# Two PSUM banks kept by one pool through the whole program, and two of three score tiles moved into them

## The chip, the cores and the metric

The kernel runs on one core of one Trainium2 chip. The metric is the device time of one launch in microseconds; the kernel before takes 1682.73 us (median of three runs, 1681.79 to 1683.66). The core's engines are named as in the profile: PE does the matmuls (PEld is its loading of weights), DVE, ACT and POOL are the vector, scalar and GpSimd engines, SP issues most of the transfers. PSUM, into which PE accumulates, has eight banks of 128 partitions by 512 fp32 values.

## The reference

A bidirectional encoder of two layers runs with the same weights on two groups of tokens (512 and 256, here handled as T = 768 columns), width 1024, fp32.

```python
for i in range(DEPTH):
    h = rms_norm(x, norm_mix[i])
    if i % N_MIXERS == 0:
        x = x + window_attention(h, attn_w_qkv[j], attn_w_o[j], attn_sink[j], band_bias, in_window)
    else:
        x = x + short_conv(h, conv_w_in[j], conv_w[j], conv_w_out[j])
    h = rms_norm(x, norm_mlp[i])
    x = x + jnp.square(jax.nn.relu(h @ mlp_w_up[i])) @ mlp_w_down[i]
    gate = jax.nn.sigmoid(rms_norm(x, norm_ple[i]) @ ple_w_gate[i])
    x = x + (p[i] @ ple_w_proj[i]) * gate
return rms_norm(x, final_norm)
```

Layer 0 has the attention: 16 heads of 64 over 4 key/value heads, blocks of 128 queries that see up to three blocks of 128 keys (|distance| at most 128), a bias per head and distance, and a learned sink logit that enters the maximum and the denominator. Layer 1 has the gated convolution of width 3. The MLP is 4096 wide.

## The kernel before, in words

**Accuracy.** Every fp32 operand is split into a high part (ACT, L83) and the rest (DVE, L84), and a product is three matmul passes: high by high, high by rest, rest by high. In the names `whi`/`wlo`, `zhi`/`zlo` are the parts of a weight, `qh`/`ql` of the queries, `khh`/`kll` of the keys, `aos` those of the heads' outputs.

**Stages.** From 0 to 73 us the inputs are projected and normalized, and keys, queries of the first heads and values are made; the pool `psK` gives three two-bank tiles for the products and a tag "S" of two banks for small things: `bp` (the bias table), `rt` (a transpose) and the six blocks of values `vp` (L653 to L655, read by ACT at L658 and DVE at L659). Then `psK` closes, `psA` opens, and attention runs to 277 us. `psA` has one two-bank accumulator `mm` (two tags, `BM`=1), three banks for score tiles (`BS`=3), one for the output `O` and two for transposes. Then `psA` closes and the pool `ps` takes all eight banks for the rest, 1400 us: four under tag A, two under C, two under B. There each product needs two banks, `both()`, and `fresh()` picks the tag from "ACAB" by a counter, `shift`.

**Attention.** 24 units (4 key/value heads by 6 blocks of 128 tokens). In a unit each of four heads has a score tile S (PE, L708 and L709), which DVE reads once, adding the bias and taking the maximum (L710). ACT exponentiates (L730), DVE and ACT scale (L736, L738), PE transposes (pt, L743), ACT and DVE split the transposes (`ph` L751, `pl` L752), and PE multiplies them with the values into O (L753, L754), from which `heads` is made (L761). Beside the units PE does the products of 512 or 256 columns that later units need (L138): the queries of later heads, `keys1`, `projected` (inputs of the second layer) and the parts of the output projection that are ready (`first_output`, `second_output`, summed into `xa` at L777). Queries are scaled, split, and sent to their places by four DMAs for each pair of heads, issued by SP (L625).

**What sets the order.** In attention and ahead of it a list scheduler at build time decides in which order each engine's instructions stand; a tile's release (its bank's last reader) enters that decision. On the chip each engine then takes its own instructions in that fixed order, and waits on semaphores. From the head of the next stage on the order is as written. That stage begins with `first_head`: six products of the last heads' outputs (L129, `group2`), each with an add into x on DVE (L847); `first_tail` has two more and the four products `pj`, whose tags are written out as A, B, C, A.

Of the kernel before, what the change touches and what calls it, by code (L numbers as in the profile page):

```python
# [11 lines left out]
F32 = mybir.dt.float32  # L12
# [3 lines left out]
PSUM = bass.MemoryType.PSUM  # L16
DRAM = bass.MemoryType.DRAM

P = 128
# [8 lines left out]
NEG = -1e30  # L28
CH = 1024

BM, BS, BO, BT, BL = 1, 3, 1, 2, 5

NA = 1

# [13 lines left out]
def trunk_kernel(ctx: ExitStack, tc: tile.TileContext, a: dict, out: bass.AP):  # L48
# [6 lines left out]
    wp = ctx.enter_context(tc.tile_pool(name="wp", bufs=2))  # L55
    stat = ctx.enter_context(tc.tile_pool(name="stat", bufs=1))
    dram = ctx.enter_context(tc.tile_pool(name="dram", bufs=1, space=DRAM))

    act.preload_act_table_set(EXP_LN)
    tmp, turn, shift = None, 0, 0  # L60


    vec = const.tile([P, 7 * KB + 3 * KB], F32, name="vec")
# [39 lines left out]
    BANKS = {"A": 4, "C": 2, "B": 2}  # L103

    def bank(tag, name):
        return psum.tile([P, 512], F32, tag=tag, name=name, bufs=BANKS[tag])

    def fresh(name="mm", n=1, tag=None):

# [371 lines left out]
    def mixer_attention():  # L481
        s1, s2 = ExitStack(), ExitStack()
        psum = s2.enter_context(tc.tile_pool(name="psK", bufs=3, space=PSUM))
# [8 lines left out]
        def pair(j, name, dt=F32):  # L492
            return main.tile([P, 2, T], dt, tag=f"x{j}", name=name)
# [40 lines left out]
        with tc.manual_schedule(engines=order):  # L534
            w0 = wp.tile([P, CH], F32, name="wraw", bufs=3)
            p0 = []
            for k in range(2):
                c = slice(512 * k, 512 * k + 512)
                nc.sync.dma_start(w0[:, c], a["proj"][0, 0, :, c])
                t = big("p")  # L540
                nc.sync.dma_start(t[:], a["p"][0, :, k, :])
                p0.append(t)
            w1 = fetch(a["proj"][0, 1])
            nc.sync.dma_start(vec[:], a["vec"][:])
            for m in range(KB):
                nc.sync.dma_start(xin(m), a["x"][m])
            wk = fetch(a["w_k"][0])
            rb = ap.tile([32, HEADS], F32, name="rb", bufs=1)
            nc.sync.dma_start(rb[:], a["rel_bias"][:])
            oh = ap.tile([32, 512], F32, tag="bias", name="oh", bufs=4)  # L550
            nc.sync.dma_start(oh[:], a["onehot"][:])
            mk = ap.tile([HEADS, 512], F32, tag="bias", name="mk", bufs=4)
            nc.sync.dma_start(mk[:], a["mask"][:].broadcast_to([HEADS, 512]))
            nc.sync.dma_start(sink[:], a["sink"][:].broadcast_to([P, HEADS]))

            hi = wp.tile([P, CH], F32R, name="whi", bufs=2)
            lo = wp.tile([P, CH], F32R, name="wlo", bufs=2)
            part0 = [], []
            for k in range(2):
                c = slice(512 * k, 512 * k + 512)  # L560
                split(hi[:, c], lo[:, c], w0[:, c])
                ph, pl = slot(10 + k, "p0h"), slot(12 + k, "p0l")
                split(ph[:], pl[:], p0[k][:])
                part0[0].append(ph[:])
                part0[1].append(pl[:])
            w0 = blocks(hi[:], 2), blocks(lo[:], 2)
            w1 = weight(None, 2, raw=w1)
            for i in range(KB):
                step(0, i, (w0, w1)[i // 4], part0, "L", i % 2)
                norm.block(i, xin(i))  # L570
                if i == 3:
                    wk = weight(None, KB, raw=wk)
                    wq = [fetch(a["w_q"][0])]

            bp = psum.tile([P, 512], F32, tag="S", name="bp", bufs=2)
            pe.matmul(bp[:HEADS, :], lhsT=rb[:], rhs=oh[:], start=True, stop=True)
            brow = tmp.tile([HEADS, 512], F32, tag="t", name="brow")
            dve.tensor_tensor(brow[:], bp[:HEADS, :], mk[:], ALU.add)
            kps = list(products(terms_of(wk, xs)))
            wq[0] = weight(None, KB, raw=wq[0])  # L580
            ss = norm.sum_squares(psum)

        with s1:
# [44 lines left out]
                        )  # L628

            rc = ap.tile([P, T // P], F32, name="rc", bufs=1)  # L630
            rt = psum.tile([P, 512], F32, tag="S", name="rt", bufs=2)
            for n in range(T // P):
                pe.transpose(rt[:, n : n + 1], r[0:1, n * P : (n + 1) * P], ident[0:1, 0:1])
            dve.tensor_copy(rc[:], rt[:, : T // P])
# [11 lines left out]
                    parts += blocks(t[:, :m], m // 256)  # L646

            def values(n):
                ps = psum.tile([P, 512], F32, tag="S", name="vp", bufs=2)
                for k in range(KB):  # L650
                    xh, xl = (xs[i][k][:, n * P : (n + 1) * P] for i in range(2))
                    wh, wl = wv[0][k], wv[1][k]
                    pe.matmul(ps[:, :256], lhsT=xh, rhs=wh, start=k == 0, stop=False)  # L653
                    pe.matmul(ps[:, :256], lhsT=xh, rhs=wl, start=False, stop=False)
                    pe.matmul(ps[:, :256], lhsT=xl, rhs=wh, start=False, stop=k == KB - 1)  # L655
                src = ps[:, :256].rearrange("p (g d) -> p g d", g=KV)
                hi, lo = vv[:, n, :, 0, :], vv[:, n, :, 1, :]
                act.activation(hi, src, AF.Copy, scale=rc[:, n : n + 1])  # L658
                dve.scalar_tensor_tensor(lo, src, rc[:, n : n + 1], hi.bitcast(F32), ALU.mult, ALU.subtract)  # L659
# [24 lines left out]
            biases = {}  # L684
            bands(0)

            def attend(g):
                heads[g] = pair(g, "heads")
                if g < KV - 1:
                    bands(g + 1)  # L690
# [2 lines left out]
                for s in SEQS:  # L693
                    hi_blk = lo_blk + s // P
                    for n in range(lo_blk, hi_blk):
# [6 lines left out]
                        for hp in range(2):  # L702
                            L = ap.tile([P, 2, 384], F32, tag="L", name="L", bufs=BL)
                            for j in range(2):
                                h = REP * g + 2 * hp + j
                                S = psum.tile([P, 512], F32, tag="S", name="S", bufs=BS)
                                q = qst[h][:, n * P : (n + 1) * P]
                                pe.matmul(S[:, :w], lhsT=q, rhs=khh[g][:, k0 * P : k0 * P + w], start=True, stop=False)  # L708
                                pe.matmul(S[:, :w], lhsT=q, rhs=kll[g][:, k0 * P : k0 * P + w], start=False, stop=True)  # L709
                                dve.tensor_tensor_reduce(  # L710
                                    L[:, j, :w],
                                    S[:, :w],
                                    bias[hp][:, j, j0 : j0 + w],
                                    1.0,
                                    sink[:, h : h + 1],
                                    ALU.add,
                                    ALU.max,
                                    accum_out=mx[:, 2 * hp + j : 2 * hp + j + 1],
                                )
                            lg.append(L)  # L720
# [261 lines left out]
    def first_tail(norm, places, output, product, ws):  # L982
# [9 lines left out]
        norm.ready = True  # L992
        c = ws[1]
        m6, m7 = KB - 1, KB // 2 - 1
        ps = [output(m) for m in (m6, m7)]
        pjs.extend(product(m) for m in range(KB // 2))
        add(m6, ps[0], xa[m6])
        norm.plain_block(m6, x(m6))
# [931 lines left out]
```

## Time and profile before

| what | us |
|---|---|
| median of three runs | 1682.73 |
| lowest, highest | 1681.79, 1683.66 |
| the profiled execution | 1684.2 |
| its span, first to last instruction | 1682.2 |
| PE busy in the span | 1645.5 (98%) |
| DVE busy | 1411.9 (84%) |
| ACT busy | 905.8 (54%) |
| stage to 73.33 us | 73.33, PE busy 66.30 |
| attention, 73.33 to 276.85 | 203.52, PE busy 197.13 |
| the rest, from 276.85 | 1405.3, PE busy 1382 |

The profiled execution lies 1.5 us above the median, and 2.0 us of it lie around the span. The granted clock of PE is 0.996 over the span. The page of the profile gives busy time by engine; the groups of waits say for how long an engine's next instruction stood and what released it; the timeline gives single instructions with that idle time in brackets; a table of windows gives busy time and clock in stretches.

### The profile page before, as it was taken

To read this page: it belongs to the slowest core of one execution; us is meant where nothing else is said; L and a number is where in the kernel's file an instruction comes from. 1 tells how busy PE (TensorE), PEld (TensorE's weight loads), DVE (VectorE), ACT (ScalarE), POOL (GpSimd) and SP (SyncE) were. 2 spreads that over 40 slices of the span, in tenths; PEclk is the share of its full clock that TensorE was granted. 3 is DMA by queue.
4 is the path that set the end of the run, shared out by engine and by line. 5 is a ranking of instruction groups with operands and counts; after the bars stand their busy time and mean duration, and the time that the engine had idled before them with its cause. 6 is when DMAs were issued, how large, how long until landed. Compare 5 with 4: busy or idle time off the path is not lost.

```text
span 1682.2 us, 24112 instructions
## 1 busy us (share of the span) xinstructions
PE 1645.5 (98%) x9410; PEld 1586.8 (94%) x9410; DVE 1411.9 (84%) x2302; ACT 905.8 (54%) x1451; POOL 20.3 (1%) x46
## 2 busy tenths in 40 slices
PE   8999999999999999999999999999999999999996
PEld 6888788999999999999999999999999999999985
DVE  6598888899999999977788787768999898998776
ACT  6377756755555455545654334545555545554544
POOL 0211000000000000000000000000000000000000
PEclk9999999999999999999999999999999999999998
DMA  8755322411221222231312222121222122122222
GB/s 262 192 152 143 92 66 74 121 63 63 76 76 64 75 76 66 73 104 63 101 60 76 76 75 76 61 66 54 73 75 76 63 76 76 63 76 88 82 76 95
DMA packets 47107, 145.64 MB, mean 87 GB/s; under 512 B 6112, under 2 KB 9184, under 8 KB 46992
## 3 DMA queue, kind: packets, MB, share of 16 engines
q1 hardware_dynamic: 45168, 139.89, 26.1%
q0 software_dynamic: 1824, 4.20, 1.2%
q8 instruction: 74, 1.21, 0.3%
q14 instruction: 41, 0.34, 0.1%
HBM read 124.14 MB, written 10.48 MB: 80 GB/s over the span
## 4 chain that ended last, share of the span: by engine, by line
PE 58%; DVE 30%; ACT 7%; issue 3%; DMA 1%; SPq 0%; DVEq 0%; ACTq 0%
PE a L476 17%; PE mm L129 9%; PE mm L138 8%; PE b L476 4%; PE B L476 4%; PE C L476 3%; DVE t L362 3%; DVE wlo L455 3%; DVE y L1031 3%; PE gate L138 3%; DVE zlo L455 2%; DVE act L395 1%; PE pt L743 1%; DVE sum L412 1%; ACT y L1034 1%
## 5 line engine op out<-in xcount | busy, mean ns | idle before, releaser
L436 ACT ACTIVATE whi<-sum 128x1024 fp32r<-128x1024 f32 x67 | 70.5, 1053 | 150.7 <-PE a L476 146.8
L1034 ACT ACTIVATE y<-y 128x768 f32<-128x768 f32 x64 | 53.7, 840 | 135.5 <-DVE y L1031 135.5
L476 PE MATMUL a<-xs,whi 128*128 128x384 f32 x624 | 121.9, 337 | 2.4 <-DVE y L1279 1.7
L476 PEld LDWEIGHTS a<-xs,whi 128*128 128x128 f32 x624 | 110.0, 188 | 3.1 <-DVE y L1279 2.0
L476 PE MATMUL a<-t,zhi 128*128 128x384 f32 x536 | 109.1, 337 | 0.0
L476 PE MATMUL a<-t,whi 128*128 128x384 f32 x536 | 108.8, 336 | 0.0
L476 PE MATMUL b<-t,zhi 128*128 128x384 f32 x536 | 108.8, 336 | 0.0
L476 PE MATMUL a<-act,whi 128*128 128x384 f32 x448 | 96.5, 337 | 0.0
L476 PEld LDWEIGHTS a<-t,whi 128*128 128x128 f32 x536 | 94.9, 188 | 0.0
L476 PEld LDWEIGHTS a<-t,zhi 128*128 128x128 f32 x536 | 94.6, 188 | 0.2 <-ACT c L1752 0.2
L476 PEld LDWEIGHTS b<-t,zhi 128*128 128x128 f32 x536 | 94.8, 188 | 0.0
L455 DVE TENSOR_TENSOR wlo<-wraw,whi 128x1024 fp32r<-128x1024 f32 x70 | 85.3, 1218 | 7.6 <-ACT whi L436 7.6
L455 DVE TENSOR_TENSOR wlo<-sum,whi 128x1024 fp32r<-128x1024 f32 x67 | 81.9, 1222 | 8.9 <-ACT whi L436 8.9
L1312 DVE TENSOR_TENSOR x<-x,a 128x384 f32<-128x384 f32 x112 | 60.7, 552 | 33.8 <-PE a L476 33.5
L436 ACT ACTIVATE zhi<-sum 128x1024 fp32r<-128x1024 f32 x67 | 71.0, 1060 | 23.0 <-DVE sum L412 23.0
L138 PE MATMUL mm<-xs_mix,whi 128*128 128x512 f32 (+1 forms) x320 | 83.0, 342 | 0.0
L455 DVE TENSOR_TENSOR zlo<-sum,zhi 128x1024 fp32r<-128x1024 f32 x67 | 81.5, 1217 | 0.0
L476 PEld LDWEIGHTS a<-act,whi 128*128 128x128 f32 x448 | 79.8, 188 | 0.0
L436 ACT ACTIVATE whi<-wraw 128x1024 fp32r<-128x1024 f32 x72 | 75.7, 1051 | 6.2 <-PE C L476 6.2
L356 ACT ACTIVATE t<-y 128x768 fp32r<-128x768 f32 x56 | 47.1, 842 | 40.6 <-DVE y L347 29.9
L476 PE MATMUL a<-xs,wlo 128*128 128x384 f32 x312 | 67.1, 336 | 0.0
L455 DVE TENSOR_TENSOR vlo<-wraw,vhi 128x512 fp32r<-128x512 f32 x67 | 46.1, 689 | 24.8 <-ACT vhi L436 24.8
(338 smaller groups left out, 4503.7 us busy)
## 6 DMA issues: line engine op xcount, KB each, us to landing
wraw<-in_up SPq DMA_DIRECT2D x64, 512.0 KB, 3.5
wraw<-in_down SPq DMA_DIRECT2D x64, 512.0 KB, 3.5
wraw<-in_w_in SPq DMA_DIRECT2D x24, 512.0 KB, 3.5
wraw<-in_gate SPq DMA_DIRECT2D x16, 512.0 KB, 3.4
pj<-pjs SPq DMA_DIRECT2D x16, 384.0 KB, 3.8
wraw<-in_w_q SPq DMA_DIRECT2D x8, 512.0 KB, 4.5
wraw<-in_w_out SPq DMA_DIRECT2D x8, 512.0 KB, 3.4
x_in<-in_x SPq DMA_DIRECT2D x8, 384.0 KB, 7.3
```

What stands on the lines that cost most here:

```text
L129: pe.matmul(t, lhsT=w, rhs=x[:, o:e], start=first and i == 0 and j == 0, stop=last and i == n - 1 and j == 2)
L138: pe.matmul(ps[:, o:e], lhsT=w, rhs=x[:, o:e], start=i == 0 and j == 0, stop=i == n - 1 and j == 2,)
L356: act.activation(t[0][:], (self.q1, self.q2)[i][:], AF.Copy)
L362: dve.tensor_tensor(lo[:], (self.q1, self.q2)[i][:], hi[:].bitcast(F32), ALU.subtract)
L395: dve.tensor_tensor(lo[:], self.q2[:], hi[:].bitcast(F32), ALU.subtract)
L412: dve.tensor_tensor(a[:, 512:], a[:, :512], r2[:, 512:], ALU.add)
L436: act.activation(hi[:], src, AF.Copy)
L455: dve.tensor_tensor(lo[:], src, hi[:].bitcast(F32), ALU.subtract)
L476: pe.matmul(ps, lhsT=a, rhs=b, start=start and i == 0, stop=i == len(terms) - 1, skip_group_check=True)
L1031: dve.scalar_tensor_tensor(t[:, o:e], src, 0.0, r[:, o:e], op, ALU.mult)
L1034: act.activation(t[:], t[:], AF.Square)
L1312: dve.tensor_tensor(t[:, o : o + H], t[:, o : o + H], f, op)
```

## The change

A pool `psB` of two banks is opened at the start of the program and never closed. `bank("B", ...)` takes from it, so the later stages' pair B, the bias table, the transpose and the blocks of values lie there. In attention two of every three score tiles lie there too, and the third in a tag "S" of one bank of `psA`; `psK`, `psA` and `ps` have six banks each. In the first product stage `shift` starts at 2 in place of 0, so the products of `first_head` take the banks B A C A B A in place of C A B A C A, and the two of `first_tail` C A in place of B A. `shift` is then set back by 2, and the rest of the program has the banks that it had.

```diff
-BM, BS, BO, BT, BL = 1, 3, 1, 2, 5
+BM, BO, BT, BL = 1, 1, 2, 5
...
+    pair_of_banks = ctx.enter_context(tc.tile_pool(name="psB", bufs=2, space=PSUM))
...
-    tmp, turn, shift = None, 0, 0
+    tmp, turn, shift = None, 0, 2
...
     def bank(tag, name):
-        return psum.tile([P, 512], F32, tag=tag, name=name, bufs=BANKS[tag])
+        pool = pair_of_banks if tag == "B" else psum
+        return pool.tile([P, 512], F32, tag=tag, name=name, bufs=BANKS[tag])
...
-            bp = psum.tile([P, 512], F32, tag="S", name="bp", bufs=2)
+            bp = bank("B", "bp")
...
-            rt = psum.tile([P, 512], F32, tag="S", name="rt", bufs=2)
+            rt = bank("B", "rt")
...
             def values(n):
-                ps = psum.tile([P, 512], F32, tag="S", name="vp", bufs=2)
+                ps = bank("B", "vp")
...
+            scores = 0
+
+            def third():
+                return psum.tile([P, 512], F32, tag="S", name="S", bufs=1)
+
             def attend(g):
+                nonlocal scores
...
-                                S = psum.tile([P, 512], F32, tag="S", name="S", bufs=BS)
+                                S = third() if scores % 3 == 1 else bank("B", "S")
+                                scores += 1
...
+        nonlocal shift
         ps = [output(m) for m in (m6, m7)]
+        shift -= 2
         pjs.extend(product(m) for m in range(KB // 2))
```

No instruction is added or removed on any engine. POOL's order is the same; those of PE, DVE, ACT and SP differ inside attention alone. The numbers behind names below are the program's own and differ by three between the two kernels; the lines of the changed kernel are up to nine lower down (L717 is L708 of before).

At the turn from values to scores, at 73 us, PE's order is the same in both: the six blocks of values, two score tiles of two heads, then the queries of the second group. What differs is the read for which the first score waits. Before it is DVE's of the sixth and last block of values (the last read of `psK`), now DVE's of the fifth, since the pair's banks take turns and the first score follows the fifth block in its bank.

The first place shown is PE about 160 us, behind the product `projected` (`mm` from `p1`), where the first scores of the third group of heads stand (`q_1872` and `q_1875`, freshly sent, are `q_1875` and `q_1878` now). Before:

```order
L754 MATMUL O_1782<-pl_1800,vv_454 128x512 [waits DVE_49]
L138 MATMUL mm_1973<-p1_1313,whi_1942 128x256
L138 MATMUL mm_1973<-p1_1312,wlo_1943 128x256
L708 MATMUL S_2035<-khh_1385,q_1682 128x256 [waits DMAHW1_49,DMAHW0_49]
L709 MATMUL S_2035<-kll_1386,q_1682 128x256
L708 MATMUL S_2040<-khh_1385,q_1872 128x256 [waits DMAHW4_49,DMAHW3_49]
L709 MATMUL S_2040<-kll_1386,q_1872 128x256
L708 MATMUL S_2044<-khh_1385,q_1875 128x256 [waits DMAHW6_49,DMAHW5_49]
L709 MATMUL S_2044<-kll_1386,q_1875 128x256
L708 MATMUL S_2093<-khh_1385,q_1679 128x384 [waits DVE_49]
```

In the changed kernel, with some thirty rows left out in the middle:

```order
L717 MATMUL S_2096<-khh_1388,q_1682 128x384 [waits DVE_49]
L717 MATMUL S_2043<-khh_1388,q_1875 128x256 [waits DMAHW6_49,DMAHW5_49]
L718 MATMUL S_2043<-kll_1389,q_1875 128x256
L718 MATMUL S_2096<-kll_1389,q_1682 128x384
L140 MATMUL mm_1986<-p1_1315,whi_1945 128x512 [waits Activation_49]
...
L140 MATMUL mm_2012<-p1_1315,wlo_1946 128x256
L717 MATMUL S_2047<-khh_1388,q_1878 128x256 [waits DMAHW7_49,DMAHW0_49]
L718 MATMUL S_2047<-kll_1389,q_1878 128x256
```

The two scores that need freshly sent queries stood next to each other, and now the second stands behind more of `projected`.

The second place is DVE about 205 to 211 us, around the split of the finished heads (`aos` from `heads`; the first row of `aos` in a list is the half whose product PE has next). Before:

```order
L752 TENSOR_TENSOR pl_2421<-pt_2415,ph_2420 128x512 [waits Activation_49]
L710 ISA L_2500,mx_2499<-S_2505,bias_1398,sink_74 128x256
...
L710 ISA L_2509,mx_2499<-S_2510,bias_1403,sink_74 128x256
...
L710 ISA L_2509,mx_2499<-S_2514,bias_1403,sink_74 128x256 [waits PE_49]
...
L84 TENSOR_TENSOR aos_2562<-heads_769,aos_2561 128x768
L761 TENSOR_TENSOR heads_2018<-O_2403,ot_2426 64x2x128 [waits Activation_49]
...
L723 TENSOR_SCALAR nm_2518<-mx_2499 128x4 [waits DVE_49]
L725 TENSOR_TENSOR es_2520<-sink_74,mx_2499 128x4
L84 TENSOR_TENSOR aos_2566<-heads_769,aos_2565 128x768
```

In the changed kernel:

```order
L761 TENSOR_TENSOR pl_2424<-pt_2418,ph_2423 128x512 [waits Activation_49]
L85 TENSOR_TENSOR ql_2493<-qt_2439,qh_2492 128x768 [waits DMAHW1_49,DMAHW0_49,Activation_49]
L719 ISA L_2512,mx_2502<-S_2517,bias_1406,sink_77 128x256 [waits PE_49]
...
L770 TENSOR_TENSOR heads_2021<-O_2406,ot_2429 64x2x128 [waits Activation_49]
...
L732 TENSOR_SCALAR nm_2521<-mx_2502 128x4 [waits DVE_49]
L734 TENSOR_TENSOR es_2523<-sink_77,mx_2502 128x4
L85 TENSOR_TENSOR aos_2569<-heads_772,aos_2568 128x768
```

The first half of the heads (`aos_2565` now) has gone ahead of this piece, and the rest of the queries (`ql`) has come into it from ahead. On PE the product that reads `aos_2569` now follows at once on the one that reads `pl_2424`; before, six score matmuls and six product matmuls stood between their equals (`pl_2421` and `aos_2566`).

The third place is PE at the first product after attention (`mm` from `aos` and the weight's parts `zhi`, `zlo`). Before:

```order
L129 MATMUL mm_3342<-aos_3304,zhi_3338 128x384 [waits DMASW5_49,DMASW4_49,DMASW6_49,DMASW3_49,DMASW7_49,DMASW2_49,DMAHW2_49,DMASW1_49,DMAHW3_49,DMASW0_49,DMAHW4_49,DVE_49,Activation_49]
L129 MATMUL mm_3343<-aos_3304,zhi_3338 128x384
L129 MATMUL mm_3342<-aos_3305,zhi_3338 128x384
L129 MATMUL mm_3343<-aos_3305,zhi_3338 128x384
L129 MATMUL mm_3342<-aos_3304,zlo_3339 128x384
```

In the changed kernel:

```order
L131 MATMUL mm_3345<-aos_3307,zhi_3341 128x384 [waits DMASW4_49,DMASW5_49,DMASW3_49,DMASW6_49,DMASW2_49,DMASW7_49,DMASW1_49,DMAHW3_49,DMASW0_49,DMAHW4_49,PE_49,Activation_49]
L131 MATMUL mm_3346<-aos_3307,zhi_3341 128x384
L131 MATMUL mm_3345<-aos_3308,zhi_3341 128x384 [waits DVE_49]
L131 MATMUL mm_3346<-aos_3308,zhi_3341 128x384
L131 MATMUL mm_3345<-aos_3307,zlo_3342 128x384 [waits DVE_49]
```

The first row no longer waits for DVE; the waits for DVE that are left stand at the rows that read the split heads (`aos_3308`) and the weight's rest (`zlo_3342`).

## The prediction

> **What bounds the kernel now.** I read first the page's busy times with the chain that ended last, then a table of windows cut at the stages, then PE's waits in attention, and the timeline at the few waits that are left.
>
> ```profile
> PE 1645.5 (98%) x9410; PEld 1586.8 (94%) x9410; DVE 1411.9 (84%) x2302; ACT 905.8 (54%) x1451; POOL 20.3 (1%) x46
> PE 58%; DVE 30%; ACT 7%; issue 3%; DMA 1%; SPq 0%; DVEq 0%; ACTq 0%
> 0.00:73.33 73.33, 66.30 (x397) 57.50 (x397) 42.19 (x53) 37.29 (x49) 9.46 (x22) 1.00 0.84 236
> 73.33:276.85 203.52, 197.13 (x1153) 166.11 (x1153) 175.90 (x527) 141.81 (x362) 8.63 (x16) 0.99 0.38 108
> ```
>
> PE is the bound: 1645.5 of the span's 1682.2 us. The chain names DVE for 30% of the span, yet PE is idle for only 36.7 us of it, so a change that neither adds nor removes work can win only from those. (A row of the windows gives the stretch, its length, the busy time with count of PE, PEld, DVE, ACT, POOL, PE's granted clock, the DMA share and GB/s.) All that is moved lies between 72 and 360 us; attention holds 203.52 - 197.13 = 6.4 us of idle PE. Its waits:
>
> ```profile
> PE S L708 <- DMA q<-ql: 2.3, 3, 1.1
> PE pt L743 <- ACT L L736: 1.3, 4, 0.6
> PE S L708 <- DVE vv L659: 1.1, 1, 1.1
> PE mm L129 <- ACT whi L83: 1.0, 1, 1.0
> PE mm L138 <- DVE aos L84: 0.8, 1, 0.8
> PE O L754 <- DVE pl L752: 0.4, 1, 0.4
> PE O L753 <- ACT ph L751: 0.2, 1, 0.2
> ```
>
> (waiting tile and line, releaser, us in all, times, longest us). Two of these waits, the third and fourth, are at a pool's opening or closing; three are for freshly sent queries.
>
> **The turn from values to scores.**
>
> ```profile
> 69.91 0.48 DVE L659 SCALAR_TENSOR_TENSOR vv<-vp,rc,vv 128x256 fp32r<-128x256 f32 x1 [1.89 <-ACT vv L658]
> 71.96 0.28 PE L655 MATMUL vp<-wvh,xs_mix 128*128 128x256 f32 x1
> 72.79 0.48 DVE L659 SCALAR_TENSOR_TENSOR vv<-vp,rc,vv 128x256 fp32r<-128x256 f32 x1 [1.18 <-ACT vv L658]
> 73.33 0.39 PE L708 MATMUL S<-khh,q 128*128 128x256 f32 x1 [1.08 <-DVE vv L659]
> ```
>
> The first score starts at 73.33, right behind DVE's last read of the last values block (72.79 + 0.48 = 73.27): it cannot use `psA` before `psK` is read out. With the change its bank is that of the fifth block, read out at 69.91 + 0.48 = 70.39, before PE ends the sixth. The wait of 1.08 goes. Next is the second score: its bank is in `psA`, over a product's banks that are long free. The queries that the two read were sent well before. The third score's bank is the sixth block's, free at 73.27, and it stands behind six product matmuls (some 1.4 us), so nothing new is late. I take **-1.1**; bounds 0 (if the loads of the first queries were really the last to come) and -1.1.
>
> **The queries' loads at 160 us, and the clock.**
>
> ```profile
> 155.29 0.93 DVE L84 TENSOR_TENSOR ql<-qt,qh 128x768 fp32r<-128x768 f32 x1
> 157.40 0.80 SPq L625 DMA_DIRECT2D q<-ql  x1
> 161.69 0.35 PE L708 MATMUL S<-khh,q 128*128 128x256 f32 x1 [0.78 <-DMA q<-ql]
> 163.29 0.36 PE L708 MATMUL S<-khh,q 128*128 128x256 f32 x1 [1.13 <-DMA q<-ql]
> 211.38 0.36 PE L708 MATMUL S<-khh,q 128*128 128x256 f32 x1 [0.41 <-DMA q<-ql]
> 157.00:160.20 3.20, 3.20 (x19) 2.56 (x18) 3.10 (x12) 1.83 (x5) 1.91 (x4) 1.00 1.04 233
> 160.20:163.60 3.40, 1.49 (x10) 1.11 (x9) 2.48 (x8) 3.15 (x12) 0.22 (x1) 1.00 1.02 298
> 163.60:167.00 3.40, 3.40 (x13) 2.91 (x12) 2.68 (x12) 1.11 (x3) 0.00 (x0) 0.51 1.04 338
> 167.00:170.00 3.00, 3.00 (x21) 2.77 (x20) 1.60 (x3) 2.23 (x6) 0.00 (x0) 0.99 0.24 97
> ```
>
> The three waits sum to 0.78 + 1.13 + 0.41 = 2.32. In the new order the second score stands some thirty PE rows later, 6 to 7 us at the matmuls' spacing, far more than its 1.13: that wait goes. The first stands about 1 us of PE work later than before, which would cover its 0.78; against it, DVE has another weight's rest and two `pl` ahead of `ql`, and SP two loads of `xa` and one of a weight ahead of the queries' loads, so they start later too. I take 0.5 for it. The third has 3.7 us more of work ahead of it, and goes. So 2.3 falls to about 0.5: **-1.7**; bounds 0 (the loads come later by all that was won) and -2.3.
>
> These two waits had a second price. In 160.20 to 163.60 PE was busy for 1.49 of 3.40 us, and in the 3.40 after it the granted clock was 0.51: 13 matmuls in 3.40 us, where the stretch behind did 21 in 3.00. At that spacing of 0.14 us, 13 matmuls take 1.9, so the drop cost 1.5. With at most 0.5 us of waits the drop should go. I don't count all of it: the profiled execution took 1684.2, the median run 1682.73, and those 1.5 may be just this drop, there in some runs alone. I take half, **-0.8**; bounds 0 and -1.5.
>
> [...]
>
> **The heads' split at 205 to 211 us.**
>
> ```profile
> 203.00:216.00 13.00, 10.75 (x62) 8.25 (x61) 12.82 (x33) 9.09 (x20) 0.00 (x0) 1.00 0.70 189
> 206.98 0.50 PE L754 MATMUL O<-pl,vv 128*128 128x512 f32 x1 [0.43 <-DVE pl L752]
> 208.65 0.95 DVE L84 TENSOR_TENSOR aos<-heads,aos 128x768 fp32r<-128x768 f32 x1
> 209.55 0.85 DVE L761 TENSOR_TENSOR heads<-O,ot 64x256 f32<-64x256 f32 x2
> 209.66 0.50 PE L138 MATMUL mm<-aos,whi 128*128 128x512 f32 x1 [0.77 <-DVE aos L84]
> 215.22 0.44 PE L743 MATMUL pt<-ident,L 128*128 128x128 f32 x2 [0.57 <-ACT L L736]
> ```
>
> Here DVE is the bound, busy for 12.82 of 13.00 us, and PE waits. The new DVE order puts the first `aos` early and `ql` behind the second `pl`. From the end of that `pl` to the end of the next `aos`, DVE has `ql` 0.93, one score 0.48, `heads` 0.85, two small rows 0.25, `aos` 0.95: 3.4 us, while PE has one matmul of 0.23 to 0.4. So PE waits some 3 us in one piece, where before it waited 0.43, 0.77 and 0.41 with work between. But DVE does the same work in either order, and behind the long wait PE's rows find the other halves ready: I take **0** for the place itself, bounds -1 and +1. The long wait could bring a clock drop of its own, like that at 163 us; half a chance at 1.5, part of it under DVE's work: **+0.5**, bounds 0 and +1.5.
>
> **Short waits elsewhere.** In the new order the multiplications with O follow more closely on their transposes in six of the units (about 0.7 us of PE work between them where 1.0 covers ACT's `ph` and DVE's `pl`), and in one unit the transposes follow 3 us closer on their scores. The rows of such waits now are 0.2 to 0.6 each. I take **+1.0**; bounds 0 and +2.0.
>
> **The end of attention.**
>
> ```profile
> 275.56 0.28 PE L138 MATMUL mm<-aos,wlo 128*128 128x256 f32 x1
> 275.76 1.06 ACT L83 ACTIVATE whi<-wraw 128x1024 fp32r<-128x1024 f32 x1 [0.74 <-PE mm L138]
> 276.33 0.41 DVE L777 TENSOR_TENSOR xa<-xa,mm 128x256 f32<-128x256 f32 x1
> 276.85 0.94 PE L129 MATMUL mm<-aos,zhi 128*128 128x384 f32 x4 [1.00 <-ACT whi L83]
> 283.19 1.02 DVE L847 TENSOR_TENSOR x<-xa,mm 128x384 f32<-128x384 f32 x2 [0.34 <-PE mm L129]
> 295.67 1.02 DVE L847 TENSOR_TENSOR x<-xa,mm 128x384 f32<-128x384 f32 x2 [0.47 <-PE mm L129]
> 359.37 1.66 PE L476 MATMUL a<-xs,whi 128*128 128x384 f32 x8 [1.68 <-DVE y L1279]
> ```
>
> The page blames `whi`; but the product reads `zhi`, and in the program its ACT wait is for the instruction that made `zhi`, done long before. What ended the wait is the other one, for DVE: the add into `xa` (276.33 + 0.41 = 276.74), the last read of `psA`'s accumulator. With the change the product's pair B is free, and it waits for PE and `zhi` alone: 1.0 goes. Of that not all reaches the end, since at 359.37 PE waits 1.68 for DVE. What starts PE earlier there helps only as far as DVE too starts earlier, and between 276 and 296 DVE waited for PE 0.34 + 0.47 = 0.81. So **-0.8**; bounds 0 (DVE sets 359) and -1.0.
>
> **Sum.** -1.1 - 1.7 - 0.8 + 0 + 0.5 + 1.0 - 0.8 = -2.9. Against the profiled execution, where the drop counts in full (-1.5), it is -3.6, so 1684.2 (span 1682.2 and 2.0 around it) goes to 1680.6. Against the median 1682.73 it gives **1679.8 us**. A difference of 0.2% (3.4 us) is about what a measurement of this kernel can tell from no change, so this is a gain just under it: the bound for faster is 1679.4, for slower 1686.1.
>
> **Rivals.**
>
> *A, only the two bank waits go* (22%): -1.1 - 0.8, and the new order takes back the rest, the queries' loads coming as late as PE does, since SP sends more ahead of them. For it: SP's queue, and 0.51 of clock with DMA busy at 1.04. Against it: the second score's thirty rows. With the short waits at +0.5 it is 1682.7 - 1.4 = 1681.3.
>
> *B, the waits go and none come* (22%): -1.1 - 2.3 - 1.5 - 1.0 = -5.9, with 0.4 back for short waits: 1677.2. For it: two score tiles free of `psA`'s tags let the scores run ahead, and PE has products to put between. Against it: the DVE order at 206 us.
>
> *C, slower: DVE's queue decides* (11%). `ql` and the `aos` halves are DVE's. If each comes later than PE by what its new place in the queue says, then the two waits at 160 us and their drop stay (0 won), the 3-us wait at the heads is added in full (+3.0, bringing a drop, +1.5), and the short waits are +1.5. Less 1.1 and 0.8 it is +4.1: 1686.8. It decides from the point where DVE has no slack in 150 to 216 us; it has 0.18 of 13.00 in the last part and 0.10 of 3.20 at 157, but 175.90 of 203.52 in the stage, which speaks against it.
>
> **How the numbers follow.** The forecast has 45%, its own range 1678 to 1681.6 by half of each term's bounds, 20% of it below 1679.4 and 25% within 0.2%. A is 22%, 20% same and 2% slower; B 22% faster; C 11%, 9% slower and 2% same. So faster 0.42, same 0.47, slower 0.11. For 8 in 10 the range takes in most of B and of A: 1676 to 1684; C and the far end of B are left out.
>
> **What would show it.** In the profile after: the first score right behind the last `vp` matmul, without a wait for `vv`; PE's waits for `q<-ql` 0.5 or less in sum, and no stretch of half clock near 160 us; one wait of some 3 us for `aos` near 205; the first L131 product within 0.3 us of attention's last matmul; `a` of L478 near 355 still waiting for `y`, by 1.7 to 1.9. Attention's length, 203.5 from first score to first product, should come out near 200.5. I am wrong if the waits for `q<-ql` stay above 1.5 (A or C), if waits on `pl`, `ph` and `L` sum to over 4 us where they are 1.9 now, or if time moves behind 360 us, where both kernels do the same.

## The result, and the profile after

The change is slower, by 0.2%: a median of 1685.39 us in 22 runs (1684.36 to 1688.61), against 1682.06 us in 22 runs of the kernel before on the same chip. The ratio is 1.0021, with a 95% interval of 1.0015 to 1.0028. That is 3.3 us, at the edge of the 0.2% that counts here, and above the upper end of the predicted range, 1684.0.

The busy times and the table of windows of the changed kernel, cut at the first score, at the first product after attention and at 366 us:

```profile
PE 1649.6 (98%) x9410; PEld 1591.8 (94%) x9410; DVE 1412.3 (84%) x2302; ACT 906.4 (54%) x1451; POOL 20.2 (1%) x46
0.00:71.17 71.17, 65.60 (x396) 57.33 (x397) 41.70 (x52) 36.33 (x47) 9.45 (x22) 1.00 0.85 240
71.17:280.89 209.72, 200.50 (x1154) 169.71 (x1153) 175.43 (x527) 142.39 (x362) 8.55 (x16) 0.97 0.36 105
```

Attention from its first score to the first product behind it takes 209.72 us where it took 203.52. The same matmuls keep PE busy for 200.50 where it was 197.13, and the granted clock in the stage is 0.97 where it was 0.99. So part of the loss is not waiting at all; PE does the same work at a lower clock. Ahead of attention 2.16 us are won (71.17 against 73.33); behind it the time is 0.3 us longer (1405.6 against 1405.3).

What PE does and waits for at the two turns (first part: timeline), and its waits from 60 to 290 us (second part; line, releaser, us, times, longest):

```profile
71.06 0.28 PE L657 MATMUL vp<-wvh,xs_mix 128*128 128x256 f32 x1
71.17 0.28 PE L717 MATMUL S<-khh,q 128*128 128x256 f32 x1
...
280.78 0.28 PE L140 MATMUL mm<-aos,wlo 128*128 128x256 f32 x1
280.89 0.85 PE L131 MATMUL mm<-aos,zhi 128*128 128x384 f32 x4
...
363.36 0.97 PE L478 MATMUL a<-xs,whi 128*128 128x384 f32 x4 [1.68 <-DVE y L1290]
```

```profile
PE S L717 <- DMA q<-ql: 4.0, 2, 2.3
PE mm L140 <- DVE aos L85: 2.8, 1, 2.8
PE pt L752 <- ACT L L745: 0.9, 1, 0.9
PE mm L140 <- ACT pjs L533: 0.7, 2, 0.6
PE O L763 <- DVE pl L761: 0.2, 1, 0.2
```

Both bank waits are gone: the first score follows the last values' matmul by 0.11 us, and the first product the last one of attention by 0.11. Of the 2.16 us at the first turn, 1.26 is the wait (1.37 us from the last `vp` to the first score before, 0.11 now) and 0.90 is not the change's: the last `vp` stands at 71.96 before and at 71.06 here, with no row moved ahead of it, and in the runs below it lies between 69.83 and 72.08.

But the waits for freshly sent queries are 4.0 where they were 2.3, and the wait for `aos` is 2.8. Behind each of the three long waits the clock falls to 0.50, for 3.4 us at 118, for 6.8 at 166 and for 3.4 at 217. These windows of the change lie ahead of the falls and inside them:

```profile
114.50:117.90 3.40, 1.66 (x12) 1.37 (x12) 1.84 (x8) 3.05 (x8) 0.00 (x0) 1.00 1.04 232
118.10:121.35 3.25, 3.25 (x10) 2.63 (x9) 2.90 (x10) 0.28 (x1) 0.00 (x0) 0.50 0.97 253
...
163.40:165.70 2.30, 0.44 (x3) 0.42 (x3) 1.00 (x3) 0.57 (x3) 0.00 (x0) 1.00 1.04 334
165.85:172.55 6.70, 6.15 (x22) 5.22 (x22) 3.10 (x10) 2.89 (x6) 0.00 (x0) 0.50 0.26 94
...
213.50:216.90 3.40, 1.06 (x6) 0.92 (x7) 3.35 (x9) 2.29 (x10) 0.00 (x0) 1.00 0.95 242
217.10:220.30 3.20, 3.20 (x12) 2.72 (x12) 2.44 (x6) 0.51 (x1) 0.00 (x0) 0.50 0.18 34
```

Before, attention had one such fall, the 3.4 us at 163.6 that the prediction shows. So half clock lasted 13.7 us where it lasted 3.4. At half the clock that is at most 5.1 us of PE's work lost on top; what shows of it is the 3.4 us by which PE is busy longer (200.50 - 197.13). The rest of the 6.2 us that attention is longer (209.72 - 203.52) is 2.8 more of idle time. The waits, without the two at the banks, went from 5.0 (2.3 + 1.3 + 0.8 + 0.4 + 0.2) to 8.6, 3.6 more, and the wait of 1.0 at attention's end is won.

At 117 us the score that waits has as much PE work ahead of it as before. PE is there sooner: it would have started the score at 115.8 (117.52 - 1.74), and it started it at 118.27 before, without a wait. The queries are not sooner, since DVE makes their `ql` later. Before, then now:

```profile
108.43 0.96 DVE L84 TENSOR_TENSOR ql<-qt,qh 128x768 fp32r<-128x768 f32 x1
118.27 0.28 PE L708 MATMUL S<-khh,q 128*128 128x256 f32 x1
```

```profile
110.14 0.93 DVE L85 TENSOR_TENSOR ql<-qt,qh 128x768 fp32r<-128x768 f32 x1
117.52 0.39 PE L717 MATMUL S<-khh,q 128*128 128x256 f32 x1 [1.74 <-DMA q<-ql]
```

So most of what was won at the first turn is lost there. Before, loads stood ahead of these sends as well (one of x and one of `in_proj`, now two of x).

Why the queries are late at 165 us shows in the sends. The table of transfers, now from 153 to 166 us, then of before from 153 to 164 (out<-in, count, KB each, median us from issue to landing):

```profile
q<-ql SPq DMA_DIRECT2D x2, 192.0 KB, 7.5
```

```profile
q<-ql SPq DMA_DIRECT2D x2, 192.0 KB, 5.5
```

The sends of `ql` take 7.5 us to land where they took 5.5. SP's own rows tell what is ahead of them now, two loads of x and one of an output weight where one load of x stood. Before, then now:

```profile
154.43 0.33 SPq L782 DMA_DIRECT2D xa<-in_x  x1
...
156.24 0.46 SPq L625 DMA_DIRECT2D q<-ql  x1
...
159.23 1.94 SPq L782 DMA_DIRECT2D xa<-in_x  x1
161.27 0.49 SPq L89 DMA_DIRECT2D wraw<-in_w_o  x1
```

```profile
154.00 0.81 SPq L791 DMA_DIRECT2D xa<-in_x  x2
154.90 0.38 SPq L90 DMA_DIRECT2D wraw<-in_w_o  x1
156.62 0.47 SPq L627 DMA_DIRECT2D q<-qh  x1
157.61 0.47 SPq L627 DMA_DIRECT2D q<-ql  x1
...
158.77 0.86 SPq L627 DMA_DIRECT2D q<-ql  x1
```

The first send of `ql` is issued 1.4 us later than before (157.61 against 156.24) and takes some 2 us longer to land. The score that needs it starts 3.6 us later (165.26 against 161.69), while PE would have been there only 2.1 us later (162.98 against 160.91). So the wait grew by 1.5 us, and it stands at the first of the two scores; the second, behind more of `projected`, no longer waits.

### The profile page after: what moved, and what is told of

It is laid out like the page before. It is cut to its first block, busy times and chain, and to the rows that moved or that the text cites. A ratio compares the mean times of both kernels' runs of the same rounds, so it can differ in the third digit from the quotient of the medians.

```text
span 1686.5 us, 24113 instructions
## 1 busy us (share of the span) xinstructions
PE 1649.6 (98%) x9410; PEld 1591.8 (94%) x9410; DVE 1412.3 (84%) x2302; ACT 906.4 (54%) x1451; POOL 20.2 (1%) x46
## 4 chain that ended last, share of the span: by engine, by line
PE 60%; DVE 29%; ACT 7%; issue 3%; DMA 1%; DVEq 0%; SPq 0%; ACTq 0%
PE a L478 17%; PE mm L131 9%; PE mm L140 8%; PE b L478 4%; PE gate L140 4%; PE B L478 3%; PE C L478 3%; DVE t L364 3%; DVE wlo L457 3%; DVE y L1042 3%; DVE zlo L457 2%; DVE act L397 1%; PE pt L752 1%; DVE sum L414 1%; ACT y L1045 1%
```

## The experiments

Three theories stood against each other. **O**: the score tiles' two kinds of banks change the order that the scheduler writes, among it SP's, and late queries cost the time. **P**: what is kept across the stages costs the time itself. **H** holds the heads' split at 215 us to be the cause. The kernel before ran beside each group; its median was 1681.9 to 1682.1.

### The tags without the pool

The kernel before, with two tags for the score tiles inside attention's pool:

```diff
-S = psum.tile([P, 512], F32, tag="S", name="S", bufs=BS)
+one = scores % 3 == 1
+S = psum.tile([P, 512], F32, tag="S" if one else "S2", name="S", bufs=1 if one else 2)
+scores += 1
```

> The kernel before, with only the score tiles' three banks put under two tags (one for every second of three, two for the others) inside attention's pool; no bank is kept across the stages, so the waits of 1.08 us at the turn from values to scores and 1.0 us behind attention stay. Theory O (the new order of the scores and loads costs the time, the pool itself saves 2): PE waits for freshly sent queries of 2 us or more again, with half clock behind them, and the time is 2 to 6 us above before, 1684 to 1688. Rival P (the tags cost nothing; what is kept across the stages costs the time): within 1 us of before. Rival H (the heads' split at 205 to 216 us costs the time): the long wait for aos of 3 us is there and the time is up by 2 to 4, with no waits for queries over 1.2.

Measured 1685.17 us, ratio 1.0022 (1.0013 to 1.0031): as slow as the change, with no bank kept across stages. So P falls. H's long wait for `aos` is not there either (0.8 us, as before). The windows about its one long wait, for `q<-ql` at 210 us:

```profile
207.00:210.40 3.40, 1.06 (x6) 0.73 (x5) 3.36 (x7) 2.17 (x9) 0.00 (x0) 1.00 1.02 240
210.40:214.00 3.60, 3.47 (x12) 2.91 (x13) 1.51 (x4) 0.51 (x1) 0.00 (x0) 0.58 0.36 102
```

The late queries are others than in the change (2.5 us at 210 and 0.4 at 160, where the change has 1.7 at 117 and 2.3 at 165). What the split into tags costs depends on which order comes of it.

### The scores held in order

The changed kernel, each score's first matmul queued on PE behind the score before it (`...` stands for a dependency that orders and adds no wait):

```diff
-pe.matmul(S[:, :w], lhsT=q, rhs=khh[g][...], start=True, stop=False)
+mm = pe.matmul(S[:, :w], lhsT=q, rhs=khh[g][...], start=True, stop=False)
+if last is not None:
+    tc.add_manual_dep(mm.ins, last.name, ..., reason="scores in order")
+last = mm.ins
```

> The changed kernel, with PE's scores held in the order in which the program writes them (each score's first matmul is queued behind the score before it; no wait is added). Banks and pools are as in the change. Theory O: the two fresh queries' scores at 160 us stand again where they did, the waits that remain are like those of before, and the two bank waits stay away: 1682 - 1.1 - 1.0 and up to 1 us more or less for the rest, 1679 to 1681.5. Rival P: as slow as the change, 1685. Rival H: the wait for aos stays at 3 us and the time within 1 us of 1685.

Measured 1686.75 us, ratio 1.0029 (1.0018 to 1.0040): this expectation failed, and no theory's numbers hold. The long waits for queries are gone, but scores held in order now wait for DVE (0.9 and 0.8), `aos` keeps 2.3 us, and half clock comes at another place too:

```profile
107.50:111.00 3.50, 2.04 (x11) 1.05 (x10) 3.21 (x9) 2.36 (x5) 1.80 (x4) 1.00 0.93 310
111.00:114.50 3.50, 2.89 (x7) 1.71 (x7) 3.02 (x7) 2.08 (x8) 2.13 (x4) 0.58 1.07 242
```

So putting PE's scores back in order does not win the time back. It brings waits of its own, so it doesn't tell what the old order alone would give.

### The loads behind the queries

The changed kernel, with the output part's loads queued on SP behind the queries needed at 160 us:

```diff
 def first_output():
-    load_part(0)
+    with tc.issue_after(sent[5].ins):
+        load_part(0)
     for j in range(2):
-        w = weight(a["w_o0"][j], 4)
+        with tc.issue_after(sent[5].ins):
+            raw = fetch(a["w_o0"][j])
+        w = weight(None, 4, raw=raw)
```

(`sent[c]` is the last send of `queries(c)`.)

> The changed kernel, with the loads of x for the output part and of the first two output weights queued on SP behind the sends of the queries that are needed at 160 us; all else as in the change. Theory O, in its narrower form (SP sends big loads ahead of the queries, and 16 DMA engines at a share of 1.04 hold the queries back): the waits for q<-ql at 117 and 165 us, 4.0 in sum, fall under 1.0, their half-clock stretches go (1.2 to 1.5 each), and the time is 5 to 7 us below the change, 1678.5 to 1680.5. If the waits come from PE and DVE coming to the queries in another order, and not from the loads: the waits stay above 2.5 and the time at 1684 to 1686. Rival H: waits for queries go but the time stays above 1683.5.

Measured 1679.88 us, ratio 0.9989 (0.9980 to 0.9998): 5.5 us below the change and 2.2 below before. Waits for `q<-ql` are 0.8 in sum and no window between 110 and 223 us shows a clock under 1.00. The edit moved rows of PE and DVE too, and the wait for `aos` fell to 1.2 with it, so the run doesn't tell O from H; runs further down part them.

### The banks of the first products put back

```diff
-tmp, turn, shift = None, 0, 2
+tmp, turn, shift = None, 0, 0
...
-        shift -= 2
```

> The changed kernel, with the first products after attention taking the banks in the order of before (C A B A C A and B A). Attention as in the change. If the bank wait behind attention is what the other order of the banks took away: the first product waits again about 1.0 us and the time is 0.8 to 1.0 above the change, 1686.2. If PE finds another product to begin with, or DVE sets the time at 360 us: within 0.3 of the change.

Measured 1686.83 us, ratio 1.0031 (1.0020 to 1.0042). That is 1.4 above the change and outside both expectations, though the interval overlaps the change's. The first product has no wait in this profile either. PE's order differs there: three steps with `zhi` and `zlo` stand in front where two did, so one of a later product has come ahead. So the shift is not what took the wait at the end away; that the pair B is not part of attention's pool is enough. The attention has the change's rows, and yet its waits for `q<-ql` are 5.3 us, not 4.0: so much do they differ from one profile to another. The longest of them at 117 us is 2.27 us where the change has 1.74, and no half clock follows it (the last section comes back to this).

### Two loads behind the first queries, and nothing else

The changed kernel, with `issue_after(sent[3].ins)` in place of `sent[5]`: two loads of x move on SP, three rows on PE, none of DVE or ACT.

```diff
-                load_part(0)
+                with tc.issue_after(sent[3].ins):
+                    load_part(0)
```

> The changed kernel, with the output part's loads queued on SP behind the sends of the queries needed at 117 us only: two loads of x, 384 KB each, move from ahead of those sends to behind them; on PE three rows move, on DVE and ACT none, and at 160 us the loads stay ahead of the queries. Theory O in the narrow form: the wait of 1.74 us for q<-ql at 117 falls to the 0.8 of the run with all loads behind, and its half-clock stretch (0.67 over 117 to 120 us, 0.76 over 120 to 123) goes; 1 to 2.5 us below the change, 1683 to 1684.4, with the waits at 165 and 215 us as in the change. If the loads ahead are not what delays the queries: the wait stays at 1.7 and the time at 1685.4.

Measured 1684.62 us, ratio 1.0013 (1.0005 to 1.0022), 0.8 below the change, just short of the 1 expected; the intervals overlap, so the time alone doesn't show it. In the profile the step is as expected: the wait at 117 us falls from 1.74 to 0.72, and its half clock is gone, while those at 165 and 213 stay:

```profile
114.00:117.50 3.50, 2.88 (x19) 2.31 (x17) 2.35 (x7) 3.47 (x11) 0.00 (x0) 1.00 1.05 212
117.50:121.00 3.50, 3.02 (x15) 2.29 (x16) 2.85 (x10) 1.64 (x3) 0.00 (x0) 1.00 1.02 326
...
163.50:167.00 3.50, 2.89 (x8) 2.12 (x9) 1.92 (x9) 1.35 (x3) 0.00 (x0) 0.56 0.79 288
213.00:216.50 3.50, 3.50 (x11) 2.92 (x12) 2.87 (x5) 1.63 (x7) 0.00 (x0) 0.50 0.27 65
```

### One load ahead again

The kernel with the loads behind the queries, with one load of x let ahead at 117 us and one at 160 us, and the rows of PE, DVE, ACT and POOL unchanged:

```diff
-with tc.issue_after(sent[5].ins):
-    load_part(0)
+load_part(0, 2)
+with tc.issue_after(sent[5].ins):
+    load_part(2, 2)
```

> The kernel with all loads behind the queries (1679.88 us), but with one load of x of 384 KB let ahead of the queries' sends at 117 us and one at 160 us; the rows of PE, DVE, ACT and POOL are the same as in that kernel. Theory O: a load of 384 KB at some 300 GB/s is 1.3 us, so the waits for q<-ql come to 2 at 117 us and up to 1.3 at 160 us, perhaps with half clock behind the first: 1 to 3.5 us above, 1681 to 1683.4. If PE's and DVE's order, and not the loads, was what made that kernel fast: 1679.9 within 0.5.

Measured 1680.74 us, ratio 0.9991 (0.9982 to 1.0000), 0.9 above 1679.88, where 1 to 3.5 was expected. The wait for `q<-ql` is 0.9, with 0.5 more at the next score, all at 117 us; at 160 us the one load is covered. No clock falls in attention. The 0.9 is not clear of noise: the two ratios (0.9991 and 0.9989) have intervals that overlap nearly whole. One load ahead of each pair of queries costs little, and these runs don't show how much.

### The kernel before, with the loads behind the queries

The edit of "The loads behind the queries" on the kernel before (there the diff is the same).

> The kernel before, with the same queuing: the output part's loads behind the sends of the queries needed at 160 us. It tells how much of the 1679.88 us is the change's own. Theory O: the waits of 0.78 and 1.13 us and the half clock behind them go, 2 to 3.5 us below before, 1678.5 to 1680, so that on equal loads the change is worth less than the 2.1 us of its two bank waits. If before's queries do not wait for the loads ahead of them: 1682 within 0.7, and the change is worth its two bank waits on equal loads.

Measured 1681.13 us, ratio 0.9996 (0.9987 to 1.0005). The waits for `q<-ql` and the half clock at 163 us are gone, but only 0.8 of the 2 to 3.5 expected reaches the time, and the interval takes in no change at all. One reason can be that the stretch of half clock isn't in every run of before alike: of its 33 runs 10 have a mean clock of 0.997 and a mean time of 1681.25 us, 18 have 0.996 and 1682.24, and 5 have 0.995 and 1683.68; its profiled execution, with the stretch, has 0.996.

### Another third of the score tiles

```diff
-S = third() if scores % 3 == 1 else bank("B", "S")
+S = third() if scores % 3 == 0 else bank("B", "S")
```

> The changed kernel, with the first of every three score tiles, and not the second, in attention's own pool. The rows of SP, POOL, and nearly all of DVE and ACT (all but 82 and 26) are as in the change, so the loads stand ahead of the queries as there. Theory O: the waits for q<-ql at 117 and 165 us stay at 3 to 5 in sum and the time at 1684.5 to 1686.5. If the place of the scores on PE sets the time: those waits change by more than 1.5 or the time leaves that range.

Measured 1684.43 us, ratio 1.0014 (1.0005 to 1.0023): the waits for `q<-ql` are 3.8 us, as O has it with SP's rows as in the change; the time is 0.1 under the stated range.

### The heads split sooner

The changed kernel, with the split of the first heads written one unit sooner; the loads up to 190 us as in the change.

```diff
-(2, 5): (begin_output, first_output),
+(2, 5): (first_output,),
...
+beside[2, 4] = (begin_output, *beside[2, 4])
```

> The changed kernel, with the split of the first heads (aos) written one unit sooner, ahead of the last queries. The order up to 190 us and the loads at 117 and 160 us are as in the change, so the waits for q<-ql there stay at 4 us in sum, with their half clock. Theory H+O (the heads' place is the other part of the loss): the wait of 2.8 us for aos and the half clock behind it (0.64 over 216 to 219.5 us) go, 3 to 4.5 us below the change, 1681 to 1682.5. Theory O alone (DVE is busy all the time there, so what is won on aos is lost on the queries behind it): within 1 us of 1685.4.

Measured 1683.5 us, ratio 1.0010 (1.0001 to 1.0019): 1.9 below the change, between the two expectations, with intervals that overlap a little. The waits for `q<-ql` stay (4.1 in three), with a clock of 0.59 at 163.5; that for `aos` falls from 2.8 to 0.4, and no half clock follows:

```profile
208.00:212.00 4.00, 3.45 (x19) 2.45 (x19) 3.89 (x9) 1.66 (x3) 0.00 (x0) 1.00 0.11 24
212.00:215.50 3.50, 2.65 (x12) 2.03 (x13) 3.50 (x12) 1.69 (x8) 0.00 (x0) 1.00 0.99 243
215.50:219.00 3.50, 3.50 (x25) 3.07 (x24) 2.35 (x10) 1.25 (x4) 0.00 (x0) 1.00 0.76 291
```

DVE is still busy all through, as O alone said. PE has three short waits there now (0.36, 0.54 and 0.50) in place of the long one, and no half clock; how the 1.9 us divide between the two isn't shown. So by the profile H has a part beside O.

### The waits filled with work

The changed kernel, with 14 matmuls ahead of the two scores that waited. They are added work and compute nothing that is used.

```diff
+if g in (1, 2) and n == 0 and hp == 1 and j == 0:
+    for _ in range(14):
+        pe.matmul(S[:, :w], lhsT=qst[h - 2][:, :P], rhs=khh[g][:, :w], start=True, stop=True)
 pe.matmul(S[:, :w], lhsT=q, rhs=khh[g][...], start=True, stop=False)
```

> The changed kernel, with 14 matmuls of 256 columns put ahead of the scores that waited at 117 and 165 us; they write, from queries that are there, into the score's own tile, which the score then overwrites: 14 x 0.115 = 1.6 us of work more at each place, 3.2 in sum. The loads are as in the change. If half clock comes from PE standing idle: the waits fall by about 1.6 each, no half clock at 117 to 124 and 163 to 174 us, and the time is at least 3 us below the change, 1680.5 to 1682.5, in spite of the work added. If half clock comes from something else there (the DMA engines at a share of 1.0, say): the clock falls as before and the time stays at 1685 or comes above.

Measured 1682.62 us, ratio 0.9999 (0.9990 to 1.0008): 2.8 below the change, with 3.2 us of matmuls more, just outside the range expected. The windows at the two places, and one at the heads:

```profile
114.00:117.40 3.40, 3.23 (x25) 2.87 (x23) 1.82 (x7) 2.96 (x8) 0.00 (x0) 1.00 1.05 219
117.40:120.90 3.50, 2.48 (x15) 1.80 (x15) 2.50 (x9) 0.71 (x3) 0.00 (x0) 1.00 0.93 247
160.00:165.30 5.30, 5.30 (x37) 4.62 (x36) 4.65 (x18) 3.75 (x13) 2.09 (x4) 1.00 1.02 274
165.30:168.00 2.70, 2.70 (x22) 2.52 (x20) 1.44 (x6) 2.21 (x6) 0.00 (x0) 1.00 1.01 262
...
204.50:208.00 3.50, 2.31 (x9) 1.16 (x9) 3.50 (x11) 3.27 (x5) 0.00 (x0) 1.00 1.02 291
208.00:211.50 3.50, 3.50 (x12) 2.97 (x13) 3.46 (x8) 2.17 (x9) 0.00 (x0) 0.54 1.01 265
```

With PE busy at 117 and 165 us the clock stays at 1.00, though the DMA engines are as full as before (1.05, 1.02). So at these two places full DMA engines brought no half clock by themselves, and of the two causes put up before the run PE's idleness is what is left. The mean clock of all its runs agrees, 0.9955 against 0.9933 in the change's. Half clock comes at 208 instead, behind a stretch with PE busy for 2.31 of 3.50. The order of later rows moved with the edit, and the wait for `aos` fell to 0.8, so its 2.8 us are not the filling's alone.

### Both edits, on the change and on the kernel before

Loads behind the queries and heads split sooner (the two diffs above together).

> The kernel with all loads behind the queries (1679.88 us), with the heads split one unit sooner as well. Theory H+O: the waits for aos there (0.94 and 0.55) and for pl (0.69) go, with no half clock, 1 to 2 us below 1679.88: 1678 to 1679. If what is won is lost on the queries' ql behind it on DVE: within 0.5 of 1679.88.

> The kernel before, with the same two edits (loads behind the queries, heads sooner). Beside the run with both edits on the change it gives the change's own worth where the orders are alike: by the two bank waits 2.0 to 2.4 us above that run, 1680 to 1681. If the score tiles' new banks are worth nothing, or cost: less than 1 us apart.

On the change: 1679.02 us, ratio 0.9979 (0.9970 to 0.9988), 2.9 below before and the fastest here; 0.9 below the loads alone, a little less than the 1 to 2 expected. On the kernel before: 1680.41, ratio 0.9987 (0.9979 to 0.9996). With the same two edits on both, the change is worth 1.4 us; expected from its two bank waits were 2.0 to 2.4. The intervals overlap, so that the 1.4 is not sure by itself, and PE's and DVE's orders still differ between the two, as those of the change and of before do.

## Why the prediction was wrong

**The turn from values to scores (-1.1): right at its place, and not kept.** The wait of 1.08 is gone; the gap shrank by 1.26. Forty-six microseconds on, the queries' sends take it back.

**The queries' loads (-1.7, worst case 0): wrong, and the step that failed first.** The waits went from 2.32 to 4.02, +1.7. The working counted PE's rows ahead of the scores and noted that SP sent two loads of x and a weight ahead of the queries, but charged that 0.5 us. At the 298 GB/s that stood in the quoted window, 2 x 384 + 512 KB take 4.4 us, 3.1 more than the one load of x before; the sends of `ql` took 2 us longer to land, and the first score waited 2.28. That the second score's wait would go was right. The working also looked only at places that waited before, and so missed the new wait of 1.74 at 117 us, where PE's gain of the turn ran into sends that come no sooner. And the bound on the bad side was 0, "all that was won is lost": a wait can grow beyond what it was.

**The clock (-0.8 and +0.5): wrong by about 4 us in the profiled executions, the largest term.** The half clock at 163 us did not go but came 2 us later and lasted twice as long, and two more stretches came: 13.7 us against 3.4, and PE busy for 3.4 us more. The median of the change is less extreme than its profiled execution (1688.33, clock 0.992). In 19 of its 22 runs the clock is 0.994, 0.993 or 0.992, with mean times of 1684.92, 1686.05 and 1687.57 us; the three others, one run each, are 1688.61 at 0.991, 1685.83 at 0.995 and 1684.49 at 0.996. So much of its spread goes with the clock. The row of before held the price: waits of 1.9 us within 3.4 had been followed by a loss of some 1.5 more. Going by it was right, and it should have priced the new waits as well.

**The heads' split (0, and the wait of 3 us): place right, price wrong.** The one long wait came as told, 2.76 us. DVE did the same work in either order, as the working said (busy for 175.4 us of attention against 175.9), but the wait in one piece was followed by half clock (0.50 for 3.4 us), and the short ones of before were not (0.43, 0.77, 0.41 and 0.57 us, with a clock of 1.00 from 203 to 216). The working had given that half a chance (+0.5). The split sooner took 1.9 us off.

**Short waits elsewhere (+1.0): too high.** `pt`, `O` and `pjs` sum to 1.8, where `pt` and `O` had 1.9 before.

**The end of attention (-0.8): right in kind, too small.** The wait is gone, the gap shrank by 1.18 and PE's wait at 360 us is the same 1.68, so all of it arrives. The reason given, that the pair B is free, holds; the shift of the products to it was not needed, as the run with the banks put back shows.

**The sum and its range.** The sum is right as added. The forecast's own range, 1678 to 1681.6, does not follow from half of each term's bounds, which give 1677.8 to 1683.5; the measured time lies above either.

**The rivals.** What happened is closest to C (11%, 1686.8): queries still late, half clock kept and a second one behind the heads. But its mechanism, `ql` and `aos` late on DVE, is only half of it. It holds at 117 us, where DVE makes `ql` 1.7 us later, and at the heads. At 165 us `ql` is 1.3 us later on DVE while PE comes 2.1 later; what makes PE wait longer there is the 2 us more to land, behind the loads on SP. That was the reason of A, which priced it as no more than the loss of what was won.

What stays open is how the 5.5 us of the loads' edit divide between 160 us and the heads, since that edit moved PE's and DVE's rows too. So the cost of the loads at 160 us is argued from the landings and not shown by a run of its own. Open as well is how idle a stretch of PE must be for half clock (see the last section).

## What to carry to other kernels

When a pool or a tag changes under a list scheduler, read the new order of the queue that issues transfers before that of the engine that waits, and price every large load that has come ahead of a small urgent one at the bandwidth of that window, at places too that did not wait before. A wait of about 2 us on PE in attention was mostly followed here by 3.4 us of half clock (in the change behind 1.74, 2.28 and 2.76 us, twice 3.4 us and once 6.8; with the banks put back not behind 2.27). By the clock of 0.50, an estimate, 3.4 us of it cost up to 1.7 us more. So price a long wait at up to double, as a chance, and prefer several short ones. Two edits of order (bulk loads queued behind urgent sends, a split written one unit sooner) took 6.4 us off the change, where the banks by themselves gave about 1.4 (not sure by itself).

## What the runs showed of the hardware

Half clock came here behind stretches in which PE was idle for a part and busy for the rest. It came after PE was busy for 1.49 of 3.40 us (before), 1.66 and 1.06 of 3.40 (the change), 1.06 of 3.40 (the two tags), 2.04 of 3.50 (the scores in order) and 2.31 of 3.50 (the filled waits).

But the share of idleness alone doesn't decide. Here are two places with no half clock behind them, the wait of 2.27 us at 117 us with the banks put back, and the change's wait of 1.68 at 363 us:

```profile
114.40:117.80 3.40, 1.17 (x9) 0.92 (x7) 1.82 (x7) 2.49 (x7) 0.00 (x0) 1.00 1.04 221
117.80:121.20 3.40, 2.97 (x14) 2.21 (x15) 1.78 (x5) 0.94 (x2) 0.00 (x0) 1.00 0.84 227
...
361.80:365.20 3.40, 1.84 (x10) 1.84 (x11) 3.40 (x6) 1.00 (x2) 0.00 (x0) 1.00 0.00 0
365.20:368.60 3.40, 3.31 (x19) 2.99 (x18) 3.37 (x5) 1.33 (x2) 0.00 (x0) 1.00 0.47 137
```

The kernel before has a wait of the same 1.68 us at 359 us, and no half clock behind it either (1.00 from 361.2 to 368).

In the profiles of before and of the change, half clock in attention lasted 3.4 us three times and 6.8 us once (at 166 in the change). At 117 us it came behind the change's wait of 1.74 us, and not behind the longer one of 2.27 with the banks put back. What parts the two isn't shown. So no border of idleness comes out of these runs, and that a wait near 2 us is followed by half clock is a chance and not a rule.
